# Attention weights, queries and keys split into two half-precision parts before they are transposed, by DMA instead of TensorE, in a decoder trunk with three mixers

## The chip, the cores and the metric

The kernel runs on one core of one Trainium2 chip. The metric is device microseconds (us) of one execution, as the median over runs; lower is better. The core has TensorE (PE in the profile, with its weight loads as PEld), VectorE (DVE), ScalarE (ACT), GpSimd (POOL) and SyncE (SP), which here only issues DMAs. Each engine takes its own instructions in order; semaphores tie them together.

## The reference, cut to what matters

Two layers, each with three mixers in parallel on the same normalised input: a short gated convolution, stick-breaking attention with eight heads of 128, and gated linear attention (GLA). One input projection of 7696 columns feeds them, one output projection adds the result to the residual. Sequence 512, model width 2048, everything in float32.

```python
def _stick_breaking(q, k, v):
    ...
    def block(i):
        start = i * SB_BLOCK
        qb = lax.dynamic_slice_in_dim(qh, start, SB_BLOCK, axis=2)
        z = jnp.einsum("bhqd,bhkd->bhqk", qb, kh)
        qpos = start + jnp.arange(SB_BLOCK)
        mask = kpos[None, :] < qpos[:, None]
        log_keep = jnp.where(mask, jax.nn.log_sigmoid(-z), 0.0)
        later = lax.cumsum(log_keep, axis=3, reverse=True) - log_keep
        w = jnp.where(mask, jnp.exp(jax.nn.log_sigmoid(z) + later), 0.0)
        return jnp.einsum("bhqk,bhkd->bhqd", w, vh)
...
def _layer(x, norm_g, w_in, conv_w, conv_b, sb_qn_g, sb_kn_g, gla_w_up, gla_b_up, gla_on_g, w_out):
    h = _rmsnorm(x, norm_g).astype(x.dtype)
    proj = h @ w_in
    ...
    q = _rmsnorm(sb_q.reshape(b, s, SB_HEADS, SB_HD), sb_qn_g)
    k = _rmsnorm(sb_k.reshape(b, s, SB_HEADS, SB_HD), sb_kn_g)
    v = sb_v.reshape(b, s, SB_HEADS, SB_HD).astype(f32)
    y_sb = _stick_breaking(q, k, v) * jax.nn.silu(sb_g.astype(f32))
    ...
    return x + mix @ w_out
```

## The kernel before

**Numbers.** Every float32 operand of a large product is written as a float16 high part and a float16 low part (the rounding error of the first), and the product is three matmuls: high with high, high with low, low with high. A weight column group of 256 comes as two float32 halves of 1 MB by DMA from SP (`fetch`, L298) into a ring of three stage buffers `st`; VectorE takes the largest magnitude (`wmax`, L309), GpSimd the maximum over partitions (`allmax`, L182), ScalarE scales and rounds the high part (`whi`, L342), VectorE makes the low part (`wlo`, L349), which frees the stage buffer. A group is prepared while the one before it is used.

**Projections.** `project_cols` (L509 to L511) gives columns on the partitions, `project_toks` (L517 to L519) tokens on the partitions, each 20 to 21 us of PE for one weight group, into two PSUM banks of the pool `psp` (three banks).

**A layer.** First GLA: values, decay, queries and keys, gates, then for each of two head pairs seven levels of a decay table and the diagonal blocks, written by predicated copies into `attd` (L710, L722), which is split into `att16` (L743, L744) and used in L766. `attd` and `att16` are one set of buffers for the whole program. Then half of the convolution, then four attention groups of two heads each, then the other half of the convolution, and the output projection.

**An attention group.** Four projections: values, gate, queries, keys. Queries and keys have tokens on the partitions. ScalarE squares each head of each token tile with a sum (L878, into a scratch tile `jk`), a reciprocal root follows, VectorE multiplies by it into the float32 tile `raw` (L886), PE transposes eight blocks of 128x128 into PSUM (L894), and the two parts are taken from PSUM: high on ScalarE (L895), low on VectorE (L896). The key gain is applied there, as one number per partition.

Each head then has two sub-blocks (`CHUNKS`), each with two query tiles of 128: the large one has tiles 3 and 2 (896 score columns in all, seven 128x128 blocks), the small one tiles 0 and 1 (384 columns, three blocks). A sub-block runs: scores on PE (L906, L908) into a PSUM pair of the pool `psz` (two pairs); on ScalarE absolute value, exponential, logarithm and rectified part (L912 to L916); on VectorE two combinations and a backward running sum (L918 to L922) and a difference (L925); the exponential on ScalarE (L926), which gives the float32 weights `w`. Then PE transposes the blocks into a second `psz` pair (L932), ScalarE takes the high part from PSUM (L934) and VectorE the low part (L935), and PE multiplies them with the values (L940). VectorE gates the result (L943), and `mixsplit` splits it for the output projection (L579, L580).

**What sets the order.** The first stretch, up to the first projection, is in an order written by hand for VectorE and ScalarE. All the rest is ordered by a scheduling pass, which lists the instructions of every queue by its own estimates of their durations, in the priority of the program's text; DMA issues take their place in SP's queue in the same way. The order is fixed when the program is built, and each queue then keeps to it.

The lines that produce the two transposes:

```python
                nT_ = wk([P, 2, 2, seq], tag, dt=F16)
                tp = bank2()
                for hh in range(2):
                    for t in range(NT):
                        T.transpose(tp[:, hh, t * P:(t + 1) * P], raw[:, t, hh * P:(hh + 1) * P], ident)
                S.activation(nT_[:, 0], tp, AF.Copy, scale=gain)
                V.scalar_tensor_tensor(nT_[:, 1], tp, gain, nT_[:, 0], ALU.mult, ALU.subtract)
```

Of the kernel before, what the change touches and what calls it, by code (L numbers as in the profile page):

```python
# [5 lines left out]
F32 = mybir.dt.float32  # L6
# [29 lines left out]
def hybrid_trunk(ctx, tc, x, norm_g, w_in, conv_w, conv_b, sb_qn_g, sb_kn_g,  # L36
# [96 lines left out]
    avg = const.tile([P, P], F32, tag="avg", name="avg")  # L133
    G.memset(avg, 1.0 / P)
    lrT = const.tile([P, seq], F32, tag="lrT", name="lrT")
    G.memset(lrT, 0.0)
    wup = const.tile([P, depth, 256], F32, tag="wup", name="wup")
    G.memset(wup, 0.0)

    attd = const.tile([P, NT, 2, P], F32, tag="attd", name="attd")  # L140
    att16 = [const.tile([P, NT, 2, P], F16, tag=f"att{i}", name=f"att{i}") for i in range(2)]
# [4 lines left out]
    G.memset(attd, 0.0)  # L146
# [26 lines left out]
    rows.append((wup[:LR], gla_w_up.rearrange("l r c -> r l c")))  # L173
# [32 lines left out]
    kg = const.tile([P, depth], F32, tag="kg", name="kg")  # L206
# [4 lines left out]
    gmx = sm(depth, "gmx")  # L211
# [4 lines left out]
    gtop = sm(depth + 1, "gtop")  # L216
# [10 lines left out]
    sel = sm(4, "sel")[:4]  # L227
# [18 lines left out]
    def layer_consts():  # L246
# [3 lines left out]
        for l in range(depth):  # L250
# [3 lines left out]
            gq = sm(2, "kg")  # L254
# [5 lines left out]
            V.tensor_scalar(kg[:, l:l + 1], gq[:, 0:1], gq[:, 1:2], 2.0 ** -10, ALU.mult, ALU.mult)  # L260
# [232 lines left out]
    for l in range(depth):  # L493
# [102 lines left out]
        tp = bank(psm, "m")  # L596
        for t, o, u in project_by_token(xh, xl, GX):
            split_v(gv[1], t, o[:, :GW])
            lr = sm(LR, "lr")
            V.tensor_scalar(lr, o[:, GW:GX], u, None, ALU.mult)  # L600
            T.transpose(tp[:LR, t * P:(t + 1) * P], lr, ident)
        V.tensor_scalar(gu[:, 1:2], u, 2.0 ** 41, None, ALU.mult)
        V.tensor_copy(lrT[:LR, :], tp[:LR, :])
        Pc = wk([P, 2, seq], "raw", 1)
        for p in range(2):
            gp = bank(psm, "m")
            T.matmul(gp, wup[:, l, p * P:(p + 1) * P], lrT, start=True, stop=True)
# [73 lines left out]
        for p in range(2):  # L681
            Pp, q_, k_ = Pc[:, p, :], gq[:, p, :], gk[:, p, :]

# [84 lines left out]
            for hh in range(2):  # L768
# [7 lines left out]
                T.matmul(ms, avg, sq, start=True, stop=True)  # L776
# [72 lines left out]
        for j in range(4):  # L849
# [21 lines left out]
            for tag, gain in (("qT", 2.0 ** 10), ("kT", kg[:, l:l + 1])):  # L871
                ps, u = project_toks(xh, xl)
                sq = sm(8, "qs")
                for t in range(NT):
                    for hh in range(2):
                        jk = wk([P, P], "jk", 1, dt=BF16)
                        o = (t % 2) * GW + hh * P
                        S.activation(jk, ps[t // 2][:, o:o + P], AF.Square, accum_out=sq[:, 2 * t + hh:2 * t + hh + 1])  # L878
# [5 lines left out]
                raw = wk([P, NT, GW], "raw", 1)  # L884
                for b in range(2):
                    V.tensor_tensor(raw[:, 2 * b:2 * b + 2, :].rearrange("p a (h c) -> p (a h) c", c=P),  # L886
                                    ps[b].rearrange("p (a c) -> p a c", c=P),
                                    rs[:, 4 * b:4 * b + 4].rearrange("p (a o) -> p a o", o=1).to_broadcast([P, 4, P]),
                                    ALU.mult)
                nT_ = wk([P, 2, 2, seq], tag, dt=F16)  # L890
                tp = bank2()
                for hh in range(2):
                    for t in range(NT):
                        T.transpose(tp[:, hh, t * P:(t + 1) * P], raw[:, t, hh * P:(hh + 1) * P], ident)  # L894
                S.activation(nT_[:, 0], tp, AF.Copy, scale=gain)  # L895
                V.scalar_tensor_tensor(nT_[:, 1], tp, gain, nT_[:, 0], ALU.mult, ALU.subtract)  # L896
                qkT.append(nT_)
            qT, kT = qkT
            for hh in range(2):
                for qtiles, regs in CHUNKS:  # L900
# [3 lines left out]
                    for t, o in qtiles:  # L904
                        for i, (a_, b_) in enumerate(((0, 0), (0, 1), (1, 0))):
                            T.matmul(z[:, o:o + (t + 1) * P], qT[:, a_, hh, tsl[t]], kT[:, b_, hh, :(t + 1) * P],  # L906
# [104 lines left out]
```

## Time and profile before

| | before |
|---|---|
| median of 3 runs | 1831.6 us (1828.81 to 1833.0) |
| the profiled execution | 1831.56 us, span 1829.4 us |
| PE busy | 1779.9 us (97%) |
| VectorE busy | 1369.4 us (75%) |
| ScalarE busy | 826.3 us (45%) |
| DMA moved | 183.73 MB, mean 100 GB/s |
| attention and second convolution half, layer 1 (284 to 667 us) | PE busy 375.98 of 383.00 us, DMA share 0.28 |
| the same, layer 2 (1194 to 1576 us) | PE busy 376.29 of 382.00 us, DMA share 0.28 |
| one attention group (377 to 473 us) | PE 95.06, VectorE 74.18, ScalarE 49.80 of 96.00 us |

Busy time counts the union of an engine's instructions. Matmuls overlap in PE's pipeline, so a matmul's listed duration is longer than the time by which it holds up the next one. In a group's line, "128x256 f16 x64 | 17.4, 272 | 4.2 <-DVE" reads: the output's shape, how many, the time in which at least one ran, the mean nanoseconds of one, the idle time of the engine just before them, and what ended it. In the timeline a line is the start, the time to the end of the last of a series, and the count.

### The profile page before, as it was taken

The numbers are of one execution on the slowest core, as the hardware profiler recorded it, in microseconds if no ns is written. First come the engines' busy times: TensorE is split into PE (matmuls) and PEld (weight loads), VectorE is DVE, ScalarE is ACT, GpSimd is POOL, SyncE is SP. The second block draws the span as 40 slices with busy tenths as digits, with TensorE's granted clock in tenths as the row PEclk, the third lists the DMA queues.
The fourth block names the chain that finished last, engine by engine and source line by source line (L and its number), as shares of the span: only waits on it lengthen the run. The fifth ranks groups of instructions, "written<-read, shape, count | busy, mean of one in ns | idle before, by whom it ended". The sixth has DMA issues, their size and how long they took to land.

```text
span 1829.4 us, 30931 instructions
## 1 busy us (share of the span) xinstructions
PE 1779.9 (97%) x13164; PEld 1272.7 (70%) x13164; DVE 1369.4 (75%) x2177; ACT 826.3 (45%) x1367; POOL 63.8 (3%) x100
## 2 busy tenths in 40 slices
PE   8999999999999999999889999999999999999999
PEld 5644456868787765788776444568686878557888
DVE  7687899778786868755486788997777878677643
ACT  6445455445464644433233454464555546443221
POOL 0000000000000000000000000000000000000000
PEclk9999999999999999999989999999999999999999
DMA  6232222232222223354423232222223232224441
GB/s 212 93 116 92 93 70 92 71 115 70 93 93 93 93 70 103 121 170 136 125 87 108 78 105 80 92 92 71 93 74 112 70 97 89 93 93 130 148 139 47
DMA packets 180858, 183.73 MB, mean 100 GB/s; under 512 B 7842, under 2 KB 179948, under 8 KB 180208
## 3 DMA queue, kind: packets, MB, share of 16 engines
q1 hardware_dynamic: 171712, 172.30, 29.8%
q10 hardware_dynamic: 9008, 9.45, 1.5%
q8 instruction: 103, 1.69, 0.4%
q14 instruction: 35, 0.29, 0.0%
HBM read 173.36 MB, written 8.39 MB: 99 GB/s over the span
## 4 chain that ended last, share of the span: by engine, by line
DVE 36%; PE 34%; DMA 21%; issue 4%; ACT 4%; POOL 0%; POOLq 0%; SPq 0%; DVEq 0%; ACTq 0%
DMA st<-in_w_in_dram 13%; DVE wl L349 12%; DVE wm L309 10%; DMA st<-in_w_out_dram 8%; PE psp L518 6%; PE psp L517 6%; PE psp L519 6%; PE psp L542 6%; PE psp L510 2%; PE psp L509 2%; PE psp L511 2%; ACT wh L342 2%; DVE tgt L672 1%; DVE attd L710 1%; DVE za L922 1%
## 5 line engine op out<-in xcount | busy, mean ns | idle before, releaser
L309 DVE TENSOR_REDUCE wm<-st 128x1 f32<-128x2048 f32 (+1 forms) x152 | 347.5, 2286 | 223.8 <-DMA st<-in_w_in_dram 117.6
L517 PE MATMUL psp<-wh,m 128*128 128x256 f16 x1664 | 453.5, 273 | 1.4 <-DVE x L959 0.9
L519 PE MATMUL psp<-wh,m 128*128 128x256 f16 x1664 | 453.3, 273 | 0.4 <-DVE wpc L188 0.4
L518 PE MATMUL psp<-wl,m 128*128 128x256 f16 x1664 | 453.4, 273 | 0.0
L349 DVE SCALAR_TENSOR_TENSOR wl<-st,ws,wh 128x2048 f16<-128x2048 f32 (+1 forms) x120 | 281.7, 2351 | 124.6 <-ACT wh L342 124.3
L342 ACT ACTIVATE wh<-st,ws 128x2048 f16<-128x2048 f32 (+1 forms) x120 | 239.9, 2001 | 185.6 <-PE psp L510 89.2
L517 PE MATMUL psp<-wh,x 128*128 128x256 f16 x768 | 209.3, 273 | 0.0
L518 PE MATMUL psp<-wl,x 128*128 128x256 f16 x768 | 209.2, 273 | 0.0
L519 PE MATMUL psp<-wh,x 128*128 128x256 f16 x768 | 209.1, 273 | 0.0
L510 PE MATMUL psp<-m,wh 128*128 128x512 f16 x512 | 194.0, 379 | 0.0
L510 PE MATMUL psp<-x,wh 128*128 128x512 f16 x512 | 194.0, 379 | 0.0
L511 PE MATMUL psp<-m,wl 128*128 128x512 f16 x512 | 194.0, 379 | 0.0
L509 PE MATMUL psp<-x,wh 128*128 128x512 f16 x512 | 194.0, 379 | 0.0
L511 PE MATMUL psp<-x,wl 128*128 128x512 f16 x512 | 194.0, 379 | 0.0
L509 PE MATMUL psp<-m,wh 128*128 128x512 f16 x512 | 193.9, 379 | 0.0
L511 PEld LDWEIGHTS <-wl 128*128 128x128 f16 x1024 | 100.2, 98 | 118.5 <-issue 2.7
L510 PEld LDWEIGHTS <-wh 128*128 128x128 f16 x1024 | 100.2, 98 | 116.8 <-issue 1.6
L509 PEld LDWEIGHTS <-wh 128*128 128x128 f16 x1024 | 100.2, 98 | 114.4 <-issue 1.1
L518 PEld LDWEIGHTS <-m 128*128 128x128 f16 x1664 | 162.8, 98 | 22.4 <-issue 2.7
L517 PEld LDWEIGHTS <-m 128*128 128x128 f16 x1664 | 162.8, 98 | 20.9 <-issue 1.5
L519 PEld LDWEIGHTS <-m 128*128 128x128 f16 x1664 | 162.8, 98 | 19.9 <-DVE m L580 1.0
L342 ACT ACTIVATE wh<-st,wsr 128x512 f16<-128x512 f32 x128 | 81.6, 709 | 128.4 <-PE psp L519 84.3
(272 smaller groups left out, 2366.1 us busy)
## 6 DMA issues: line engine op xcount, KB each, us to landing
st<-in_w_in_dram SPq DMA_DIRECT2D x120, 1024.0 KB, 5.2
st<-in_w_out_dram SPq DMA_DIRECT2D x32, 1024.0 KB, 5.8
x<-in_x_dram SPq DMA_DIRECT2D x4, 1024.0 KB
qT<-in_x_dram ACTq DMA_DIRECT2D x8, 512.0 KB, 4.0
qT<-xs ACTq DMA_DIRECT2D x8, 512.0 KB, 3.6
xs<-x SPq DMA_DIRECT2D x14, 256.0 KB, 2.4
out_dram<-kT SPq DMA_DIRECT2D x14, 256.0 KB, 2.1
g<-in_norm_g_dram ACTq DMA_DIRECT2D x2, 512.0 KB
```

What stands on the lines that cost most here:

```text
L309: V.tensor_reduce(peak[i][:, h:h + 1], staged[i][h][:, :, :n], AX.XY, ALU.max, apply_absolute_value=True)
L342: S.activation(wh[:, ks, :n], staged[i][h][:, ks, :n], AF.Copy, scale=s_)
L349: V.scalar_tensor_tensor(wl[:, ks, :n], staged[i][h][:, ks, :n], s_, wh[:, ks, :n], ALU.mult, ALU.subtract)
L509: T.matmul(o, wh[:, kk, cs], xh[:, :, k, :], start=st_, stop=False)
L510: T.matmul(o, wh[:, kk, cs], xl[:, :, k, :], start=False, stop=False)
L511: T.matmul(o, wl[:, kk, cs], xh[:, :, k, :], start=False, stop=en)
L517: T.matmul(o, ah[:, t, k, :], wh[:, kk, :n], start=st_, stop=False, skip_group_check=True)
L518: T.matmul(o, ah[:, t, k, :], wl[:, kk, :n], start=False, stop=False, skip_group_check=True)
L519: T.matmul(o, al[:, t, k, :], wh[:, kk, :n], start=False, stop=en, skip_group_check=True)
L542: T.matmul(o[:, :n], a_[:, t, k, :], w[k // HK][part][:, k % HK, :n], start=i == 0 and k == 0, stop=i == 2 and k == KT - 1)
L672: V.tensor_tensor(lo, eh, hi, ALU.subtract)
L710: V.copy_predicated(attd.rearrange("p t h (b s j) -> p (t h) b s j", s=2, j=h)[:, :, :, 1, :], masks[:, li, :].rearrange("p (o b s j) -> p ...
```

## The change

The attention weights are no longer transposed in float32 by PE. ScalarE and VectorE split `w` in place, with queries on the partitions, into the high part `wh` (tag `sh`) and the low part `wl` (tag `sl`), one buffer each; four transposing DMAs from SP per sub-block (one for each part and query tile, of one to four 128x128 blocks) write them into `th` and `tl`, two buffers each, laid out by key tile. The value matmuls read those. Queries and keys are treated alike: `raw` is split into `hi` and `lo` (tags `qh` and `ql`, one buffer each, so the keys' parts come after the queries' DMAs), and one transposing DMA of eight blocks moves each part. Per group of two heads that makes 4 + 16 DMAs, 160 in the program.

Since the split now comes ahead of the transpose, the key gain lies along the free axis: `kg` becomes a 128x128 matrix per layer, made with one matmul, and is multiplied in with the reciprocal root, by eight operations on 128 columns instead of two on 512. The squares go into `raw` instead of `jk`.

The rest is about room in SBUF. `avg` shrinks to a column, `lrT` and `wup` become tiles of the work pool (`wup` loaded once per layer), `attd` takes the tag `zw` (two buffers, which attention weights and a convolution tile also use) and is cleared by GpSimd for each head pair, `att16` takes the tags `sh` and `sl`, and the output stretch's scratch tile takes `sh`.

```diff
@@ -130,20 +130,13 @@
-    avg = const.tile([P, P], F32, tag="avg", name="avg")
+    avg = const.tile([P, 1], F32, tag="avg", name="avg")
     G.memset(avg, 1.0 / P)
-    lrT = const.tile([P, seq], F32, tag="lrT", name="lrT")
-    G.memset(lrT, 0.0)
-    wup = const.tile([P, depth, 256], F32, tag="wup", name="wup")
-    G.memset(wup, 0.0)
-
-    attd = const.tile([P, NT, 2, P], F32, tag="attd", name="attd")
-    att16 = [const.tile([P, NT, 2, P], F16, tag=f"att{i}", name=f"att{i}") for i in range(2)]
+
...
-    G.memset(attd, 0.0)
...
-    rows.append((wup[:LR], gla_w_up.rearrange("l r c -> r l c")))
...
-    kg = const.tile([P, depth], F32, tag="kg", name="kg")
+    kg = const.tile([P, depth, P], F32, tag="kg", name="kg")
...
-            V.tensor_scalar(kg[:, l:l + 1], gq[:, 0:1], gq[:, 1:2], 2.0 ** -10, ALU.mult, ALU.mult)
+
+            dg = wk([P, P], "e")
+            V.tensor_scalar(gq[:, 0:1], gq[:, 0:1], gq[:, 1:2], 2.0 ** -10, ALU.mult, ALU.mult)
+            V.tensor_scalar(dg, ident, gq[:, 0:1], None, ALU.mult)
+            T.matmul(pps[:, (l + 1) * P:(l + 2) * P], ones.to_broadcast([P, P]), dg, start=True, stop=True)
+            V.tensor_copy(kg[:, l, :], pps[:, (l + 1) * P:(l + 2) * P])
...
         tp = bank(psm, "m")
+        wup = wk([LR, 2 * P], "ga")
+        nc.sync.dma_start(wup, gla_w_up[l])
...
-        V.tensor_copy(lrT[:LR, :], tp[:LR, :])
+        lrT = wk([LR, seq], "e")
+        V.tensor_copy(lrT, tp[:LR, :])
         for p in range(2):
...
-            T.matmul(gp, wup[:, l, p * P:(p + 1) * P], lrT, start=True, stop=True)
+            T.matmul(gp, wup[:, p * P:(p + 1) * P], lrT, start=True, stop=True)
...
         tsl = [slice(t * P, (t + 1) * P) for t in range(NT)]
         for p in range(2):
             Pp, q_, k_ = Pc[:, p, :], gq[:, p, :], gk[:, p, :]
+            attd = wk([P, NT, 2, P], "zw")
+            G.memset(attd, 0.0)
+            att16 = [wk([P, NT, 2, P], "s" + c, 1, F16) for c in "hl"]
...
-                T.matmul(ms, avg, sq, start=True, stop=True)
...
             qkT = []
-            for tag, gain in (("qT", 2.0 ** 10), ("kT", kg[:, l:l + 1])):
+            for tag, gain in (("qT", None), ("kT", kg[:, l, :])):
                 ps, u = project_toks(xh, xl)
                 sq = sm(8, "qs")
+                raw = wk([P, NT, GW], "raw", 1)
                 for t in range(NT):
                     for hh in range(2):
-                        jk = wk([P, P], "jk", 1, dt=BF16)
                         o = (t % 2) * GW + hh * P
-                        S.activation(jk, ps[t // 2][:, o:o + P], AF.Square, accum_out=sq[:, 2 * t + hh:2 * t + hh + 1])
+                        S.activation(raw[:, t, hh * P:(hh + 1) * P], ps[t // 2][:, o:o + P], AF.Square, accum_out=sq[:, 2 * t + hh:2 * t + hh + 1])
                 u2 = sm(1, "qu2")
                 V.tensor_scalar(u2, u, u, 1.0 / P, ALU.mult, ALU.mult)
                 rs = sm(8, "qr")
                 rsqrt(rs, sq, u2, 8, "q")
                 V.tensor_scalar(rs, rs, u, None, ALU.mult)
-                raw = wk([P, NT, GW], "raw", 1)
-                for b in range(2):
-                    V.tensor_tensor(raw[:, 2 * b:2 * b + 2, :].rearrange("p a (h c) -> p (a h) c", c=P),
-                                    ps[b].rearrange("p (a c) -> p a c", c=P),
-                                    rs[:, 4 * b:4 * b + 4].rearrange("p (a o) -> p a o", o=1).to_broadcast([P, 4, P]),
-                                    ALU.mult)
-                nT_ = wk([P, 2, 2, seq], tag, dt=F16)
-                tp = bank2()
-                for hh in range(2):
+                if gain is None:
+                    for b in range(2):
+                        V.tensor_tensor(raw[:, 2 * b:2 * b + 2, :].rearrange("p a (h c) -> p (a h) c", c=P),
+                                        ps[b].rearrange("p (a c) -> p a c", c=P),
+                                        rs[:, 4 * b:4 * b + 4].rearrange("p (a o) -> p a o", o=1).to_broadcast([P, 4, P]),
+                                        ALU.mult)
+                else:
                     for t in range(NT):
-                        T.transpose(tp[:, hh, t * P:(t + 1) * P], raw[:, t, hh * P:(hh + 1) * P], ident)
-                S.activation(nT_[:, 0], tp, AF.Copy, scale=gain)
-                V.scalar_tensor_tensor(nT_[:, 1], tp, gain, nT_[:, 0], ALU.mult, ALU.subtract)
+                        for hh in range(2):
+                            o = (t % 2) * GW + hh * P
+                            V.scalar_tensor_tensor(raw[:, t, hh * P:(hh + 1) * P], ps[t // 2][:, o:o + P],
+                                                   rs[:, 2 * t + hh:2 * t + hh + 1], gain, ALU.mult, ALU.mult)
+
+                top = 2.0 ** 10 if gain is None else 1.0
+                hi, lo = (wk([P, NT * GW], "q" + c, 1, F16) for c in "hl")
+                S.activation(hi, raw, AF.Copy, scale=top)
+                V.scalar_tensor_tensor(lo, raw.rearrange("p t c -> p (t c)"), top, hi, ALU.mult, ALU.subtract)
+                nT_ = wk([P, 2, NT, 2, P], tag, dt=F16)
+                for i, part in enumerate((hi, lo)):
+                    nc.sync.dma_start_transpose(nT_[:, i].rearrange("p t h c -> p (t h) c"), part)
                 qkT.append(nT_)
             qT, kT = qkT
...
-                            T.matmul(z[:, o:o + (t + 1) * P], qT[:, a_, hh, tsl[t]], kT[:, b_, hh, :(t + 1) * P],
+                            T.matmul(z[:, o:o + (t + 1) * P], qT[:, a_, t, hh, :], kT[:, b_, :t + 1, hh, :],
...
-                    wT = bank2().rearrange("p a c -> p (a c)")
-                    for kt, ko, n in regs:
+
+                    wh, wl = (wk([P, zw], "s" + c, 1, F16) for c in "hl")
+                    S.activation(wh, w, AF.Copy, scale=2.0 ** 14)
+                    V.scalar_tensor_tensor(wl, w, 2.0 ** 14, wh, ALU.mult, ALU.subtract)
+                    th, tl = (wk([P, NT, 2, P], "t" + c, 2, F16) for c in "hl")
+                    for src, dst in ((wh, th), (wl, tl)):
                         for t, o in qtiles:
-                            if t >= kt:
-                                c0 = ko + n - (q0 + 2 - t) * P
-                                T.transpose(wT[:, c0:c0 + P], w[:, o + kt * P:o + (kt + 1) * P], ident)
-                    wh, wl = (wk([P, zw], "w" + c, 1, F16) for c in "hl")
-                    S.activation(wh, wT[:, :zw], AF.Copy, scale=2.0 ** 14)
-                    V.scalar_tensor_tensor(wl, wT[:, :zw], 2.0 ** 14, wh, ALU.mult, ALU.subtract)
+                            nc.sync.dma_start_transpose(dst[:, :t + 1, t - q0, :], src[:, o:o + (t + 1) * P])
                     op = bank(psm, "m")[:, :2 * P]
                     hs = slice(hh * P, (hh + 1) * P)
                     for i, (kt, ko, n) in enumerate(regs):
-                        for a_, b_ in ((vh, wh), (vh, wl), (vl, wh)):
-                            T.matmul(op[:, 2 * P - n:], a_[:, kt, hs], b_[:, ko:ko + n], start=i == 0 and b_ is wh and a_ is vh,
+                        for a_, b_ in ((vh, th), (vh, tl), (vl, th)):
+                            T.matmul(op[:, 2 * P - n:], a_[:, kt, hs], b_[:, kt].rearrange("p a c -> p (a c)")[:, 2 * P - n:],
+                                     start=i == 0 and b_ is th and a_ is vh,
                                      stop=i == len(regs) - 1 and a_ is vl, skip_group_check=True)
...
-                    jk = wk([P, GW], "xjk", 1, dt=BF16)
+                    jk = wk([P, GW], "sh", 1, dt=F16)
                     S.activation(jk, dst[:, i, :], AF.Square, accum_out=ssq[:, t + i, gi:gi + 1])
```

More of the change, by code (lines that the diff above doesn't have):

```diff
@@ L210, in hybrid_trunk @@
     onmax = const.tile([P, depth], F32, tag="onmax", name="onmax")
-    gmx = sm(depth, "gmx")
+    gmx = sm(depth, "gmx", 1)
     V.tensor_reduce(gmx, ngr, AX.X, ALU.max, apply_absolute_value=True)
@@ L215, in hybrid_trunk @@
     T.transpose(gps[:depth, :P], gmx, ident)
-    gtop = sm(depth + 1, "gtop")
+    gtop = sm(depth + 1, "gtop", 1)
     V.tensor_reduce(gtop[:depth, depth:], gps[:depth, :P], AX.X, ALU.max)
@@ L226, in hybrid_trunk @@
     gb = []
-    sel = sm(4, "sel")[:4]
+    sel = sm(4, "sel", 1)[:4]
     V.tensor_scalar(sel, ident[:4, :4], xsc[:4, 0:1], None, ALU.mult)
@@ L252, in layer_consts @@
             V.tensor_scalar(onmax[:, l:l + 1], onmax[:, l:l + 1], float(P) ** 0.5, None, ALU.mult)
-            gq = sm(2, "kg")
+            gq = sm(2, "kg", 1)
             V.scalar_tensor_tensor(gq[:, 0:1], pcol("qn", l), float(P) ** -0.5, pcol("kn", l), ALU.mult, ALU.mult)
@@ L775, in hybrid_trunk @@
                 ms = bank(psm, "m")
-                T.matmul(ms, avg, sq, start=True, stop=True)
+                T.matmul(ms, avg.to_broadcast([P, P]), sq, start=True, stop=True)
                 r_ = wk([P, seq], "e")
```

## The prediction

> **What bounds the kernel now.** I read the totals and the clock first, then the chain of waits, then the groups by shape, then the order of TensorE (PE) around one transpose, and last the DMA issues.
>
> ```profile
> span 1829.4 us, 30931 instructions
> PE 1779.9 (97%) x13164; PEld 1272.7 (70%) x13164; DVE 1369.4 (75%) x2177; ACT 826.3 (45%) x1367; POOL 63.8 (3%) x100
> PEclk9999999999999999999989999999999999999999
> q1 hardware_dynamic: 171712, 172.30, 29.8%
> DVE 36%; PE 34%; DMA 21%; issue 4%; ACT 4%; POOL 0%; POOLq 0%; SPq 0%; DVEq 0%; ACTq 0%
> ```
>
> PE is busy for 97% of the span at nearly its full clock. The chain spends much of its length on the weight pipeline (VectorE and DMA), but that pipeline stands level with PE and not ahead of it: the projections' matmuls wait 1.4 us and 0.4 us in all. So PE time saved counts, if nothing new makes PE wait. The shapes that the change touches, and the only PE waits beside them:
>
> ```profile
> L517 PE MATMUL psp<-wh,m 128*128 128x256 f16 x1664 | 453.5, 273 | 1.4 <-DVE x L959 0.9 <-DVE kT L959 0.5
> L932 PE MATMUL psz<-ident,zw 128*128 128x128 f32 x160 | 23.2, 276 | 2.8 <-ACT zw L926 2.6
> L894 PE MATMUL psz<-ident,raw 128*128 128x128 f32 x128 | 19.3, 273 | 0.3 <-DVE raw L886 0.3
> L940 PE MATMUL psm<-wl,v 128*128 128x256 f16 x64 | 17.4, 272 | 4.2 <-DVE bpc L188 3.2 <-DVE wl L935 1.1
> ```
>
> A duration of 273 ns is a pipelined one. What an instruction costs PE is the step to the next start:
>
> ```profile
> 407.02 0.38 PE L510 MATMUL psp<-x,wh 128*128 128x512 f16 x1
> 407.23 0.93 PE L932 MATMUL psz<-ident,zw 128*128 128x128 f32 x7
> 408.00 0.33 PE L906 MATMUL psz<-kT,qT 128*128 128x128 f16 x3
> 412.71 0.27 PE L940 MATMUL psm<-wh,v 128*128 128x256 f16 x1
> ```
>
> Seven transposes take from 407.23 to 408.00, 0.110 us each; a 512-column matmul steps 0.216 us and a 256-column one 0.109 us. The value matmul that uses these transposes follows at 412.71, after other work.
>
> ```profile
> st<-in_w_in_dram SPq DMA_DIRECT2D x120, 1024.0 KB, 5.2
> out_dram<-kT SPq DMA_DIRECT2D x14, 256.0 KB, 2.1
> L298 SPq DMA_DIRECT2D st<-in_w_in_dram x124: 367/368/8201, 1.6 to 1593.1; - x124
> ```
>
> One issue holds SyncE's queue (SP) for 0.37 us. A weight load lands after 5.2 us, and the quickest sizeable DMA after 2.1 us.
>
> **What goes.** 160 transposes of the attention weights and 128 of queries and keys, 288 x 0.110 = 31.7 us of PE. The PE waits around them (2.8 + 0.3 + 4.2 = 7.3 us) go too, or turn into the new ones below. Together -39.0 us.
>
> **What comes.** 160 transposing DMAs on SP: per group of two heads (eight groups in all), four of eight 128x128 blocks for q and k, and sixteen of one to four blocks for the four attention sub-blocks (14 or 6 blocks each, 10 in the mean). The trace of before holds no transposing DMA, so a block is bounded. 32 KB is 128 rows of 256 bytes, eight on each of 16 engines. A 1 KB packet costs 0.298 x 16 x 1829.4 us / 171712 = 51 ns; a quarter of it, eight times, is the lower end, 0.10 us per block. [...] The fixed part is the 2.1 us landing.
>
> [...]
>
> **The wait that replaces them.** All of it is off PE; the question is whether PE arrives first. In the changed order I added up PE's steps between the first value matmuls (L949) of successive sub-blocks: 8.1 us in the mean (5.5 to 12.9), where before it was 13.4 us, since the score matmuls of two sub-blocks now go together and no longer share PSUM with the transposes. PE takes its instructions in order, so a sub-block must be delivered every 8.1 us. Its loop, through the single buffers sh and sl: the low part on VectorE (rows of 1.086 and 0.549 us, mean 0.82), an issue 0.37, a weight load in front, 2.1 us to land, and 10 blocks x 0.30 = 3.0. In SP's new order a weight load stands among or just ahead of the four transposes in about 2.6 of 4 sub-blocks, 0.65 x 5.2 = 3.4 us. The loop is 9.7 us, 1.6 us too long, and three spacings in each of eight groups make 24 x 1.6 = +38.4 us. The first sub-block of a group has 28 to 31 us of PE work behind its scores, which covers it. Behind the high part that waits for its buffer stand ScalarE's exponentials and weight rounding (L342 before); behind a waiting transpose on SP stand the next weight loads, used a projection (192 x 0.109 = 20.9 us of PE) later, so I cost their delay at nothing; if that cover went, each load would stop VectorE's maximum (L309) and then PE.
>
> Keys: squares 8 x 0.473 (276 + 197 ns), reciprocal root 1.5, eight multiplications with the gain at 0.28 (nearest row: 282 ns for 128 columns) instead of two at 0.683, high 1.1, low 1.3, issue 0.4, landing 2.1 + 16 x 0.30 less the 1.3 by which the high part is ahead: 3.8 + 1.5 + 2.3 + 1.1 + 1.3 + 0.4 + 5.6 = 16.0 us. PE has 15.0 us of other matmuls between the key projection and the first scores: 8 x 1.0 = +8 us. Queries have a projection more of cover, 20 us, and cost nothing. VectorE gains 8 x 0.28 - 2 x 0.683 = 0.9 us per group; it is busy 74.2 of 96 us there, so it is hidden.
>
> The rest: a matrix of key gains per layer (a matmul and a few small operations each) +1 us at most, at the start. Four clears of the diagonal buffer on GpSimd at 0.99 us, ahead of the weight maxima, while POOL is 3% busy: nothing. The diagonal buffer now has two copies and its halves share tags with the attention; the waits before L677 are 11.3 us, so between -5 and +3, taken as 0.
>
> **Sum.** -39.0 + 38.4 + 8 + 1 = +8.4 us on 1831.56 us (span 1829.4 and 2.2 outside it; the median of the runs is 1831.6): 1840 us.
>
> **Rivals.** (1) The transposes hide, and it is faster. At 0.10 us per block the loop is 0.82 + 0.37 + 3.4 + 2.1 + 1.0 = 7.7, under 8.1, and the key chain 12.8, under 15: 1831.6 - 38 = 1794; spacings under 7.7 us (half of them, by about 0.6) and waits of the old kind give back some 15 us, so 1795 to 1827, middle 1810. For it: the DMA engines are 28% busy in the attention stretch. It decides as soon as a block costs under about 0.15 us.
> [...]
> (3) Gain and waits cancel within 0.2%, which is about what a measurement of this kernel can tell from no change (3.7 us): it needs the loop at 9.4 us or so, a point between the forecast and (1).
> That the change does not do what it says is excluded: the changed order of instructions holds 160 transposing DMAs and no transposes at those places.
>
> **Chances.** Forecast (1836 to 1890) 0.40, rival (1) 0.30, rival (2), 1890 to 1950 and beyond, 0.20, rival (3) 0.10. Faster 0.30, same 0.10, slower 0.60. The range reaches into (1) and up to (2): 1806 to 1944; the forecast's own is 1836 to 1890.
>
> **What would show it.** Right: L894 and L932 have no successors on PE; idle time before L949 of 30 to 50 us and before L916 of 5 to 15, released by DMA; transposes of four blocks landing in 3 to 9 us; the GLA and output stretches unchanged within 5 us. Rival (1): those idle times under 15 us. [...] Wrong altogether: VectorE or the weight loads as the releaser of most new PE waits.

## The result, and the profile after

| | before | after |
|---|---|---|
| median | 1831.08 us, 6 runs (1827.62 to 1833.43) | 1839.39 us, 6 runs (1836.8 to 1842.5) |
| ratio to before, 95% interval | | 1.0047 [1.0031, 1.0063] |
| profiled execution (span) | 1831.56 us (1829.4) | 1841.45 us (1839.4) |

The changed kernel is 0.47% slower. Its page, first the totals, then the DMA queue of the weights and transposes (packets, MB, share of the engines' time), then the chain of work that ended last:

```profile
span 1839.4 us, 30743 instructions
PE 1758.7 (96%) x12880; PEld 1241.4 (67%) x12880; DVE 1373.5 (75%) x2229; ACT 812.9 (44%) x1367; POOL 75.7 (4%) x101
...
q1 hardware_dynamic: 250576, 191.20, 36.3%
...
DVE 35%; PE 30%; DMA 24%; issue 5%; ACT 4%; POOL 1%; SPq 1%; DVEq 0%; POOLq 0%; ACTq 0%
```

TensorE is busy for 21 us less and the span is 10 us longer, so some 31 us more of it are time in which TensorE runs nothing. The groups by shape say where that stands (out<-in, shapes, count, busy us, mean ns, idle us before them and its releaser):

```profile
L514 PE MATMUL psp<-wh,m 128*128 128x256 f16 x1664 | 454.7, 273 | 5.0 <-DVE x L969 2.7 <-DVE raw L897 2.3
L949 PE MATMUL psm<-th,v 128*128 128x256 f16 x128 | 28.9, 282 | 20.0 <-DMA th<-sh 17.5 <-DVE e L953 2.5
L949 PE MATMUL psm<-tl,v 128*128 128x256 f16 x64 | 18.3, 285 | 8.9 <-DMA tl<-sl 8.7
L916 PE MATMUL psz<-kT,qT 128*128 128x512 f16 x48 | 14.3, 378 | 6.0 <-DMA kT<-ql 4.6 <-DMA kT<-qh 1.4
```

The float32 transposes (L932 and L894 before) have no successors. The value matmuls (L949, before L940) are released by the transposing DMAs, and so are the first scores (L916). The same from the side of the waits (engine, tile and line waited in, what released it, us in total, times, longest):

```profile
PE psm L949 <- DMA th<-sh: 17.5, 10, 4.1
PE psm L949 <- DMA tl<-sl: 8.7, 9, 2.6
ACT sh L939 <- DMA th<-sh: 12.2, 5, 2.8
ACT qh L902 <- DVE raw L897: 53.4, 8, 8.4
DVE wm L306 <- DMA st<-in_w_in_dram: 186.2, 86, 6.8
PE psp L514 <- DVE raw L897: 2.8, 2, 2.3
PE psp L514 <- DVE x L969: 2.7, 2, 2.4
```

The line of the weights in the kernel before:

```profile
DVE wm L309 <- DMA st<-in_w_in_dram: 117.6, 70, 6.7
```

ScalarE now waits for the single buffer `sh` until its transpose has been read (12.2 us), and, eight times some 7 us, for the keys with their gain (L897). VectorE's maxima wait 186.2 us for weights, where it was 117.6 us, but no wait of this size on TensorE follows from it: before L514, the first part of a projection, TensorE waits 5.5 us for VectorE, which empties the PSUM banks in the multiplication by the key gain (L897) and in the update of the output (L969).

To make a ledger, I summed TensorE's steps from start to start by the median step of each kind of matmul, and called the rest of the time between the first and the last matmul gaps (7.6 to 7.8 us of the span lie outside). The steps fall from 1758.3 to 1728.1 us: -30.2, of it -31.4 for the transposes and some +1.2 for the small matmuls of the key gains and the GLA gates. The gaps rise from 63.5 to 103.5 us: +40.0. Of the gaps after, 35.4 us stand before L949, 7.0 before L916 and 8.3 between the third and first part of a projection (L516 to L514; 1.8 us before). The old waits around transposes and value matmuls, some 11.5 us, are gone. Net +9.9, the difference of the spans is 10.0.

Not all of the gaps are waits. The granted TensorE clock is 0.995 in the mean of the first profile and 0.992 in this one, and the difference lies in short stretches at half clock, in which a 256-column matmul steps 0.21 us instead of 0.109. One of them follows a wait for a transposing DMA (start us, duration, engine, line; in brackets the idle time before; below, the stretch itself: window, its length, busy time of PE, PEld, DVE, ACT and POOL, granted clock, DMA share, GB/s):

```profile
440.60 0.27 PE L516 MATMUL psp<-wh,x 128*128 128x256 f16 x1
443.41 0.37 PE L949 MATMUL psm<-th,v 128*128 128x256 f16 x1 [2.54 <-DMA th<-sh]
444.97 0.42 PE L514 MATMUL psp<-wh,x 128*128 128x256 f16 x1
445.18 0.42 PE L515 MATMUL psp<-wl,x 128*128 128x256 f16 x1
443.40:446.80 3.40, 3.39 (x18) 2.47 (x19) 3.37 (x7) 1.00 (x3) 0.00 (x0) 0.50 0.00 0
```

Between 340 and 760 and between 1270 and 1670 us the changed kernel has five such stretches, from 344.4, 443.4, 627.7, 1330.8 and 1556.1 us, 20.5 us together; the kernel before has none there. Four of them begin within 2.2 us of the end of a wait of 2.5 to 4.1 us before L949, the first behind a wait of 2.1 us for ScalarE; two waits of 2.3 and 2.4 us before L514 have none behind them, so what sets the clock back is not shown. The slower steps in the five add up to some 8.8 of the 40.0 us. Where both kernels have half clock, between the two layers, the kernel before has 17.1 us of it (from 912.2 and 949.7) and the changed one 10.2 (from 921.2), some 5.4 us of slower steps against 2.8, so over the whole span the clock makes some 6 of the 9.9 us.

The place agrees: compared at the same projection matmul, the changed kernel is 0.5 us late at 367 us, when the first attention begins; 6.0 us late at 801 us, when it has ended (the last value matmuls of the layer run at 740 to 750 us, later than the 667 us of the table ahead of the prediction); 5.8 at 1275 us, after the second GLA; 14.0 at 1562 us, near the end of the second attention; 10.6 at 1710 us and 10.0 at the end. Only the attention stretches lose time.

SyncE's own queue around one attention sub-block (start us, us to the end of the last, engine, line, operation, count):

```profile
408.51 1.19 SPq L944 DMA_TRANSPOSE th<-sh  x1
409.83 0.49 SPq L295 DMA_DIRECT2D st<-in_w_in_dram  x1
410.38 1.26 SPq L944 DMA_TRANSPOSE th<-sh  x1
411.68 2.73 SPq L944 DMA_TRANSPOSE tl<-sl  x2
416.66 2.42 SPq L944 DMA_TRANSPOSE th<-sh  x2
422.20 0.37 SPq L295 DMA_DIRECT2D st<-in_w_in_dram  x1
423.27 2.41 SPq L944 DMA_TRANSPOSE tl<-sl  x2
```

A weight load holds the queue for 0.37 to 0.49 us, a transposing DMA for about 1.2. All issues of line L944, and of the queries' line (duration in ns: least, median, most; first and last start):

```profile
L944 SPq DMA_TRANSPOSE th<-sh x64: 1120/1236/2262, 408.5 to 1645.7; - x64
L944 SPq DMA_TRANSPOSE tl<-sl x64: 1120/1237/2504, 411.7 to 1648.3; - x64
...
DMA to landing us min/median/max: 2.3/4.0/6.7
```

```profile
L906 SPq DMA_TRANSPOSE qT<-qh x8: 1232/1259/1382, 353.5 to 1562.0; - x8
```

One block or eight, the issue takes 1.2 us: the medians are 1172 ns for one block, 1237 for two, 1252 for three, 1192 for four and 1233 for eight. From the start of the issue to landing, the DMAs of the attention weights take 4.0 us in the median, but the trace holds the landing of only 13 of the 128. Nine of these were issued within 5 us behind a load of projection weights, and took 4.7 us in the median; the other four took 2.9. In the second profile of this kernel (e9 below) it is 4.7 us for nine and 2.6 for four.

### The profile page after: what moved, and what is told of

It reads as the page before. It is cut to its first block, busy times and chain, and to the rows that moved or that the text cites. A ratio compares the mean times of both kernels' runs of the same rounds, so it can differ in the third digit from the quotient of the medians.

```text
span 1839.4 us, 30743 instructions
## 1 busy us (share of the span) xinstructions
PE 1758.7 (96%) x12880; PEld 1241.4 (67%) x12880; DVE 1373.5 (75%) x2229; ACT 812.9 (44%) x1367; POOL 75.7 (4%) x101
## 4 chain that ended last, share of the span: by engine, by line
DVE 35%; PE 30%; DMA 24%; issue 5%; ACT 4%; POOL 1%; SPq 1%; DVEq 0%; POOLq 0%; ACTq 0%
DMA st<-in_w_in_dram 16%; DVE wl L346 11%; DVE wm L306 8%; PE psp L514 6%; PE psp L515 6%; PE psp L516 6%; PE psp L539 5%; DMA st<-in_w_out_dram 5%; DVE za L932 2%; ACT wh L339 2%; PE psp L506 1%; PE psp L507 1%; DMA tl<-sl 1%; PE psp L508 1%; DMA th<-sh 1%
## 5 line engine op out<-in xcount | busy, mean ns | idle before, releaser
L306 DVE TENSOR_REDUCE wm<-st 128x1 f32<-128x2048 f32 (+1 forms) x152 | 347.7, 2288 | 296.6 <-DMA st<-in_w_in_dram 186.2
L514 PE MATMUL psp<-wh,m 128*128 128x256 f16 x1664 | 454.7, 273 | 5.0 <-DVE x L969 2.7
L516 PE MATMUL psp<-wh,m 128*128 128x256 f16 x1664 | 454.4, 273 | 0.0
L514 PE MATMUL psp<-wh,x 128*128 128x256 f16 x768 | 211.0, 275 | 0.6 <-DVE raw L897 0.6
L516 PE MATMUL psp<-wh,x 128*128 128x256 f16 x768 | 210.7, 275 | 0.0
L514 PEld LDWEIGHTS <-m 128*128 128x128 f16 x1664 | 163.3, 98 | 25.7 <-issue 3.1
L516 PEld LDWEIGHTS <-m 128*128 128x128 f16 x1664 | 163.3, 98 | 19.5 <-issue 0.3
```

The costliest lines, as they stand in the source:

```text
L306: V.tensor_reduce(peak[i][:, h:h + 1], staged[i][h][:, :, :n], AX.XY, ALU.max, apply_absolute_value=True)
L514: T.matmul(o, ah[:, t, k, :], wh[:, kk, :n], start=st_, stop=False, skip_group_check=True)
L516: T.matmul(o, al[:, t, k, :], wh[:, kk, :n], start=False, stop=en, skip_group_check=True)
```

## The experiments

Twelve runs, in four sets, each on one chip. The kernel before is in every set, and the sets differ in it:

| | runs | the kernel before, median |
|---|---|---|
| first measurement | before, after | 1831.08 us |
| chip A | e1 to e4 | 1840.59 us |
| chip B | e5 to e8 | 1839.44 us |
| chip C | e9 to e11 | 1840.48 us |
| chip D | e12 | 1830.12 us |

So kernels are compared with each other within a set, and a ratio to before is one for that set's chip. The chip of the first measurement is not on record and none of the others was used twice, so whether the chip makes the level is not shown. Ratios between two experiments have an interval from resampling their runs.

**e1: the room changes alone.** TensorE transposes everything again, and the key gain is one number per partition again; the changes of buffers (`attd`, `att16`, `wup`, `lrT`, `avg`, the scratch tiles) stay.

```diff
-                for i, part in enumerate((hi, lo)):
-                    nc.sync.dma_start_transpose(nT_[:, i].rearrange("p t h c -> p (t h) c"), part)
...
+                        T.transpose(tp[:, hh, t * P:(t + 1) * P], raw[:, t, hh * P:(hh + 1) * P], ident)
...
-                            nc.sync.dma_start_transpose(dst[:, :t + 1, t - q0, :], src[:, o:o + (t + 1) * P])
...
+                                T.transpose(wT[:, c0:c0 + P], w[:, o + kt * P:o + (kt + 1) * P], ident)
```

> All transposes on TensorE again, with the room changes kept (small avg, lrT and wup in the work pool, attd and att16 in shared tags, squares into raw). Theory W (the waits for the DMAs ate the gain): no DMA waits and no gain, so before within 0.2%, 1828 to 1835 us. Rival R (the room changes cost the time, the transposes by DMA are a gain as intended): 1845 us or more.

Measured 1832.21 us, 0.9956 [0.9941, 0.9970] of before on chip A. That is 8.4 us under the kernel before there, and within 1.2 us of the 1831.08 us that the kernel before had in the first measurement; its ledger (steps 1758.9, gaps 63.9 us) is that of the first profile of before (1758.3, 63.5). So rival R, 1845 us or more, is out: the room changes cost nothing. Whether they gain is open, since the 8.4 us may be what chip A adds to the kernel before and not to this one.

**e2: only the attention weights by DMA; e3: only queries and keys by DMA.** Each undoes one half of e1's diff above.

> Only the attention weights go by DMA; queries and keys are transposed by TensorE again. Theory W: 17.4 us of transposes and some 9 us of old waits go, some 35 us of waits before the value matmuls come: +6 to +12 us on before, 1837 to 1843 us. If instead the keys make the loss (rival K): 1810 to 1822 us.

> Only queries and keys go by DMA; the attention weights are transposed by TensorE. Theory W: 14.0 us of transposes go, about 7 us of waits before the scores and some 5 us before the projections (the longer key multiplication) come: 1826 to 1832 us. Rival K (the keys make the loss): 1840 us or more.

e2 took 1837.79 us, 0.9986 [0.9975, 0.9996] of before, and 1.0030 [1.0017, 1.0047] of e1 on the same chip: +5.6 us; the time is within theory W's range, though under the kernel before on this chip and not 6 to 12 us over it. Its steps are 17.2 us shorter than e1's, its gaps 27.7 longer; that is +10.5, since the profiled execution took 1842.31 us, 4.5 above its median. e3 took 1851.50 us, 1.0062 [1.0048, 1.0076] of before, and 1.0105 [1.0092, 1.0120] of e1: +19.3 us, for a saving of 13.3 us in steps. That is above what theory W allowed and in rival K's range: I had not expected the queries and keys to be the costlier half. Lines of the waits of e1, and then of e3:

```profile
ACT kT L893 <- PE psz L892: 32.6, 8, 7.0
```

```profile
ACT qh L902 <- DVE raw L897: 44.1, 8, 6.5
ACT qh L902 <- DVE raw L889: 24.8, 8, 4.6
PE psz L943 <- ACT zw L936: 11.2, 14, 1.8
PE psz L916 <- DMA kT<-ql: 5.7, 4, 1.6
```

In e1 ScalarE waits for TensorE's transposes of the keys (32.6 us; 3.1 us for the queries). In e3 it waits for VectorE's multiplications instead, 44.1 + 24.8 = 68.9 us. Those waits stand in ScalarE's queue ahead of the attention's exponentials, and TensorE, which in this kernel still transposes the weights, waits for these: in the ledger the gaps before that transpose grow from 3.5 to 14.4 us, before the values from 5.3 to 10.7, and before the scores, where the DMA is the releaser, from 1.2 to 6.3. So the waits that name the DMA are the smaller part of what this half costs. That ScalarE's waits cause the rest is argued here from the order of its queue; e6 tests it in part.

**e4: one DMA for each part of a sub-block.** Both halves by DMA as in the changed kernel, but a part's seven or three blocks go in one transposing DMA instead of two, 64 issues for the weights instead of 128.

```diff
-                    th, tl = (wk([P, NT, 2, P], "t" + c, 2, F16) for c in "hl")
+                    th, tl = (wk([P, 8, P], "t" + c, 2, F16) for c in "hl")
                     for src, dst in ((wh, th), (wl, tl)):
-                        for t, o in qtiles:
-                            nc.sync.dma_start_transpose(dst[:, :t + 1, t - q0, :], src[:, o:o + (t + 1) * P])
+                        nc.sync.dma_start_transpose(dst[:, :zw // P, :], src)
...
```

The value matmuls and the gating after them follow the new layout.

> The whole change, but each part of a sub-block goes in one DMA of seven or three blocks instead of two DMAs of one to four: the same bytes in half as many DMAs. An issue holds SP for 1.1 to 1.25 us whatever the number of blocks. Theory I (the issues in SP's queue set the delivery): the waits before the value matmuls, 28.9 us, fall by a third to a half, 1822 to 1831 us. Theory L (the landing and the bytes set it): within 3 us of the changed kernel, 1836 to 1843 us.

1835.43 us, 0.9973 [0.9963, 0.9984] of before: between the ranges of the two theories, and in neither. Lines of its waits:

```profile
PE psm L956 <- DMA tl<-sl: 18.5, 18, 2.4
PE psm L956 <- DMA th<-sh: 2.4, 4, 1.0
ACT sh L939 <- DMA th<-sh: 4.7, 2, 2.5
```

Against the changed kernel, the wait for the high part falls from 17.5 to 2.4 us and that for the low part rises from 8.7 to 18.5: it is now the low part that TensorE mostly waits for, 18 times against 4. Together they fall from 26.2 to 20.9 us, by a fifth, where theory I asked for a third or more. The issue of a DMA of seven or three blocks still takes 1.22 us in the median, so half as many issues are half the time in SyncE's queue. And the halves don't add up: with queries and keys already by DMA (e3), sending the weights by DMA too, in this merged form, is 16.1 us faster on the same chip, 0.9913 [0.9892, 0.9933], while in e2 the weights by DMA cost 5.6.

**e5: the kernel before as its own control.**

> The kernel before, unchanged, as a control of the chip's own level in this series: 1827 to 1834 us, beside 1836 to 1843 us for the changed kernel.

1840.40 us, above the 1827 to 1834 that I had expected, but 1.0006 [0.9996, 1.0015] of before on chip B: no difference, as it must be. Its profile (span 1837.9 us) beside the first one of the same kernel (1829.4) shows the difference of the sets: steps 1758.5 against 1758.3 us, gaps 71.8 against 63.5. At equal instructions the lateness grows in many small steps, the largest of 1.6 us, to 4.3 us at 350 us and 8.4 at 800. Some 2 us of it come between 340 and 350 us, where this profile has a stretch of 3.4 us at half clock (from 347.6) and the first has none.

**e6: queries and keys by DMA, without the key gain.** As e3, but the keys are treated like the queries, two operations of 512 columns instead of eight of 128. It leaves out the multiplication by the key gain, and only that.

```diff
-            for tag, gain in (("qT", None), ("kT", kg[:, l, :])):
+            for tag, gain in (("qT", None), ("kT", None)):
```

> Queries and keys by DMA, attention weights by TensorE, and the key gain left out: keys are treated as queries, two multiplications on 512 columns instead of eight on 128. Theory G (the eight multiplications hold up VectorE and, behind it, ScalarE, which waits 44 us for them in its queue): 10 to 18 us under the 1851.5 us of the kernel with the gain, 1833 to 1842 us. Rival N (the detour of the queries and keys by DMA itself): within 4 us of 1851.5 us.

1842.36 us, at the upper end of theory G's range and 9 us from rival N's; 1.0018 [1.0008, 1.0029] of before on chip B, where e3 had 1.0062 [1.0048, 1.0076] on chip A, whose level was 1.2 us higher. So about 0.44%, 8 us, of e3's excess hangs on the gain; gaps 86.5 us against 96.1. The waits of ScalarE for the split of queries and keys fall from 68.9 to

```profile
ACT qh L902 <- DVE raw L889: 54.5, 16, 5.5
```

that is by 14.4 us. In the ledger the gaps before the transposes of the weights, 14.4 us in e3, are down to some 3.6, as in e1, while those before the values rise from 10.7 to some 19.3: the sum of ScalarE's waits is not by itself what TensorE pays. Two chips are compared here, so the size is good to a few us at best.

**e7: the value matmuls later in TensorE's order.** As the changed kernel, with lower priority for L949, which puts them 4.1 us of PE work later in the mean; **e8: the same with the merged DMAs of e4.**

```diff
-                    for i, (kt, ko, n) in enumerate(regs):
...
+                    with tc.high_priority(-480 if j < 3 else -335):
+                        for i, (kt, ko, n) in enumerate(regs):
...
```

> The changed kernel with one thing moved: the value matmuls get a later priority, so that the scheduling pass puts them 4.1 us of TensorE work further behind their scores in the mean (37.7 instead of 33.6 us); the DMAs are the same. Theory J (the pass puts the value matmuls where it believes the DMAs have landed, and they land later): the idle time before the value matmuls falls from 28.9 us to under 12 us and the time by 10 to 20 us, 1820 to 1830 us. Rival S (the delivery is too slow as a rate, so the wait only moves): idle time over 20 us, 1834 to 1843 us.

> Both: each part of a sub-block in one DMA, and the value matmuls 6 us of TensorE work later than in that kernel (38.1 instead of 32.1 us). Theory J: idle before the value matmuls under 6 us, 1814 to 1824 us, under the kernel before. Rival S: 1832 to 1838 us, as with the merged DMAs alone.

e7 took 1843.25 us, 1.0017 [1.0008, 1.0026]; e8 1839.38 us, 1.0001 [0.9985, 1.0017]. Neither came near theory J's times (1820 to 1830 and 1814 to 1824 us). By its ratio e7 is not clear of the changed kernel (1.0024 [1.0012, 1.0036] in e9 below), and e8 lies above e4, though each pair was measured on two chips. The waits of e7 before the value matmuls:

```profile
PE psm L950 <- DVE e L954: 12.3, 8, 3.3
PE psm L950 <- DMA th<-sh: 10.3, 4, 3.2
PE psm L950 <- DVE pmix L182: 3.9, 2, 3.3
PE psm L950 <- DMA tl<-sl: 2.9, 3, 1.9
```

The waits for DMA fall from 26.2 to 13.2 us, and 16.2 us of waits for VectorE take their place: the values' product has a single PSUM bank, which VectorE's gating (L954, 12.3 of them) must have emptied before the next sub-block's matmuls begin. That wait has mostly changed its name.

**e9: the changed kernel again, on chip C; e10: weights alone by DMA, merged; e11: the changed kernel with a second pair of buffers for the split weights.** e10 is e2 with e4's edit. In e11 the small sub-blocks use the buffers `qh` and `ql`:

```diff
-                    wh, wl = (wk([P, zw], "s" + c, 1, F16) for c in "hl")
+                    wh, wl = (wk([P, zw], ("s" if q0 else "q") + c, 1, F16) for c in "hl")
```

> The changed kernel, unchanged, beside the kernel before in this series, whose level (1840 us) lies 9 us above that of the first measurement. If the change costs the same here, a ratio of 1.003 to 1.006 to the kernel before, 1846 to 1851 us.

> Only the attention weights go by DMA, each part of a sub-block in one DMA; queries and keys by TensorE, room changes kept. From the ratios to the kernel before so far (room changes alone 0.9956, weights alone 0.9986): theory I (the number of issues sets the delivery) expects some 5 to 10 us under the weights alone, a ratio of 0.993 to 0.996, 1827 to 1833 us, as fast as TensorE's transposes or faster. Theory L (bytes and landing): 0.9975 to 0.9995.

> The changed kernel with a second pair of buffers for the split attention weights: the small sub-blocks use those of the queries and keys. Theory B (the loop through the single buffers, as the prediction has it, sets the delivery): the waits for DMAs before the value matmuls fall by more than half, and the time by 8 us or more on the changed kernel. Theory I (the issues in SP's queue): those waits fall by less than a quarter, and the time is within 4 us of the changed kernel.

e9: 1844.41 us, 1.0024 [1.0012, 1.0036]; slower than before on a second chip, though by less than in the first measurement. e10: 1831.78 us, 0.9951 [0.9937, 0.9966] of before, and 0.9932 [0.9909, 0.9948] of the changed kernel beside it, -12.6 us; that is theory I's range (0.993 to 0.996) and not theory L's, against 0.9986 for e2, with twice the issues, on chip A. e11: 1835.51 us, 0.9971 [0.9959, 0.9982], and 0.9952 [0.9929, 0.9969] of the changed kernel, -8.9 us. Waits of e10, then of e11:

```profile
PE psm L944 <- DMA tl<-sl: 16.3, 18, 2.5
PE psm L944 <- DMA th<-sh: 1.6, 3, 0.9
```

```profile
PE psm L949 <- DMA tl<-sl: 10.4, 10, 2.3
PE psm L949 <- DMA tl<-ql: 8.1, 4, 3.0
PE psm L949 <- DMA th<-sh: 6.2, 6, 4.2
PE psm L949 <- DMA th<-qh: 2.0, 2, 1.6
```

In e11 ScalarE's wait for the buffer (12.3 us in e9) is gone, as the second pair must bring it; but TensorE's waits before the values are still 26.7 us, against 29.6 in e9. The time speaks for the loop through the single buffers, the waits against it as the main cause. The profiled executions took 1841.48 and 1851.26 us, each the longest of its kernel, but they differ by about as much as the medians. Of the 9.7 us between their spans (1839.5 and 1849.2) some 3.5 stand before L949 in the ledger's way of counting, and some 6.4 before L514, where the listed idle time falls from 4.7 us (VectorE's L969 and L897) to 0.2. So in these two executions most of the gain came before the projections and not before the values.

**e12: e10 with the second pair of buffers.**

> Weights alone by DMA, each part of a sub-block in one DMA, and a second pair of buffers for the split parts, so that the large and the small sub-blocks don't share one; queries and keys on TensorE, the room changes kept. It is the kernel of e10 with the second pair of e11, and asks whether the buffer loop still costs anything once SyncE issues two DMAs per sub-block instead of four. Theory B (the loop through the single buffers counts by itself, as the 0.5% between e9 and e11 suggests): the ratio to before falls from e10's 0.995 to 0.988 to 0.992, 1819 to 1826 us on the level of 1840.5, and TensorE's waits before the value matmuls from 17.9 us to under 10. Theory O (the in-order queues of TensorE and SyncE set what is left; the scheduling pass puts the value matmuls as close behind the landing as it estimates it): 0.9935 to 0.9965, 1828.5 to 1834, waits of 13 to 22 us.

1837.13 us, 1.0038 [1.0023, 1.0053] of before, on chip D. Both theories miss: the ratio is far above either, and even the time itself, on a chip where the kernel before takes 1830.12 us, is above what both gave at 1840.5. Waits:

```profile
PE psm L944 <- DMA tl<-sl: 18.8, 13, 3.6
PE psm L944 <- DMA th<-sh: 5.1, 7, 1.5
PE psm L944 <- DMA tl<-ql: 2.6, 2, 1.4
```

26.5 us of waits for DMA stand before the values, where e10 had 17.9, although the scheduling pass has set the values of successive sub-blocks further apart (9.5 us of PE work in the mean against 7.9). So with merged DMAs the second pair does not shorten TensorE's waits, and why e11 was faster stays open. Since e10 and e12 ran on different chips, and the kernel before differs by 10 us between these, their difference of 5.4 us is no measure of the pair.

**The best found.** e1 and e10 are under the kernel before on the chips where they ran (levels of 1840.59 and 1840.48 us), and e10 under the changed kernel as well, which ran beside it but not beside e1. Neither ran where the kernel before takes 1830 us, and their 1832 us would be no gain there, if they took the same.

## Why the prediction was right, and where it was not

The time, 1840 us forecast and 1839.4 measured, and its sign were right, and so was the mechanism in the main: the transposes leave TensorE, and it waits for DMA before the values and the first scores. The sum came out better than its terms, partly by luck.

*What goes, -39.0.* Steps of -31.4 us for the transposes (0.109 us each, predicted 0.110), and 11.5 us of old waits instead of 7.3: -42.9. (With the 35.4, 7.0 and 6.5 us below this makes +6.0 of the +9.9. The matmuls that make the key gains add 0.4 and those of the GLA gates 0.8; the slower steps at half clock between the three parts of a projection, as far as they are not in the 6.5, add some 4.5; smaller waits elsewhere take some 2 back.)

*The values, +38.4.* The ledger has 35.4 us, the listed idle time 28.9, just under the 30 to 50 that I had named. But the loop of 9.7 us was put together from wrong pieces. The step that failed is "an issue 0.37": a transposing DMA holds SyncE for 1.24 us, and a sub-block has four. No run shows the 0.30 us that this loop and the key chain take for a block, nor a block so dear that it would give the 1944 us at the top of the range. Measured, a block is nearer the 0.10 us of the lower end: its 256-byte packets took 18 ns in the median in the trace's records, eight per engine, 0.14 us; by the page of the profile, the queue's share grew by 6.5% of 16 engines, 0.065 x 16 x 1839.4 / 78864 more packets = 24 ns, 0.19 us a block. And the weight load in front, costed at 3.4 us, holds the queue for under 0.5 us in the timeline above; what it may cost besides is the later landing, 4.7 against 2.9 us. With measured pieces: low part 0.82, three issues 3.7, and from the start of the last issue to its landing 4.0: 8.5 us, not 9.7; against 8.1 us of work that leaves 24 x 0.4 = 10 us. The trace has another split: of the gaps before L949 some 23 us stand before the second to fourth sub-blocks of the groups, where I had 38.4, and some 12 before the first ones, which I had called covered (the longest, 4.1 us of listed idle, ends at 1332.9 us). So 38.4 came near 35.4 by luck. That this loop is what sets the wait is not shown: e11 speaks for it with its time, e11's waits and e12 against.

*The keys, +8.* 7.0 us of gaps before L916, in the range named. That VectorE's work is "hidden" is the step that fell in the experiments: e3 and e6 put the price of the gain's eight operations at about 8 us (343 ns each, where I took 282), through ScalarE's queue. I had looked at VectorE's busy time, not at who stands in line behind the operation that waits for it. That size was measured in kernels whose TensorE still transposes the weights, and across two chips. How much of it the changed kernel itself pays isn't known; its ScalarE waits there as long (53.4 us), and its TensorE waits 2.8 us before L514 until L897 has emptied the PSUM banks of the key projection.

*The weights' delay, "at nothing".* VectorE's waits for weights grew by 68.6 us, and nothing on TensorE shows them. The gaps from L516 to L514 did grow by 6.5 us, but some 2.1 of these are steps at half clock, and the listed idle before L514 names VectorE's L897 and L969, not the weights.

*The clock, no term.* The forecast read "nearly its full clock" off the profile of before and left it there. The half clock made some 6 of the +9.9 us of the spans; by this estimate the same waits at full clock would have come to some +4. A forecast of +8.4 without this term was lucky in its size.

*The rest, +1.* Nothing in the first profile speaks against it, and e1 shows that the room costs nothing.

*The rivals.* Rival (1) was to decide "as soon as a block costs under about 0.15 us". The block came out at 0.14 to 0.19, and it did not decide: the fixed time of the issue, which I had set at 0.37, counts as well, by e4 and e10, where half as many issues went with less time. A block took one and a half to two times the 0.10 us from 1 KB packets, and an issue 1.24 us against the 0.37 of a weight load. The issue of one block took 1172 ns in the median and that of eight 1233, so in this trace it was paid per DMA and not per block. Rival (2) had 1890 us and more, which the time misses by some 50 us; the longest landing that the trace holds was 6.7 us. Rival (3) is excluded by the interval of the first measurement, 1.0031 to 1.0063; on chip C (e9) 0.2% lies within the interval.

## What to carry to other kernels

In these runs a transposing DMA held its queue for about 1.2 us, whether it had one block (1172 ns in the median) or eight (1233): count the issues, and try as many blocks with each as the layout allows (e4 and e10 were faster so; e12, with a second pair of buffers, was not). Putting the consumers later in the order did not help by itself: in e7 the wait went over to the single PSUM bank behind them (12.3 us). When work moves off the bounding engine, look for who stands in the queue behind each new wait, on every engine it passes; the busy time of that engine says nothing about it. Look at the granted clock in short stretches, too: here the clock fell to half for 3.4 to 6.8 us beside waits of 2.1 to 4.1 us, and 256-column matmuls stepped 0.21 us instead of 0.109. And a difference of half a per cent is a difference only against a kernel measured beside it.

## What the runs showed that I had not expected

The same program took 1830 to 1831 us in two sets and 1839 to 1841 us in three, at nearly the same granted clock (0.995 and 0.996 in the two profiles) and with the same steps on TensorE; the 8 us are many small waits, beside the stretch at half clock named under e5. The DMA lines of the two profiles of the kernel before (first measurement, then chip B) differ little:

```profile
q1 hardware_dynamic: 171712, 172.30, 29.8%
...
st<-in_w_in_dram SPq DMA_DIRECT2D x120, 1024.0 KB, 5.2
```

```profile
q1 hardware_dynamic: 171712, 172.30, 30.2%
...
st<-in_w_in_dram SPq DMA_DIRECT2D x120, 1024.0 KB, 5.4
```

The same packets take a little longer and a weight load lands 0.2 us later. Whether that is the cause, or the order in which small delays meet, stays open. The changed kernel differed less (1839.4 and 1844.4 us), which is why its ratio went from 1.0047 to 1.0024.
